# The rows of h and the middle tiles shifted by 32 bytes against the weights, in a two-layer hybrid trunk

## The chip, the cores and the metric

The kernel runs on one core of a Trainium2 chip. The metric is device time in microseconds (us), measured over several executions of which the median counts; one further execution is recorded by the hardware profiler, and all profile lines come from that one. The engines are called as in the profile: PE (TensorE, matmuls), PEld (TensorE, loading of weights), DVE (VectorE), ACT (ScalarE), POOL (GpSimd) and SP (SyncE, which here issues the DMAs).

## The reference

The model has two layers, 256 tokens and a width of 2048. Layer 0 mixes tokens by retention with 8 heads, layer 1 by a short gated convolution; each is followed by a SwiGLU feed-forward part with 5632 middle columns. Every sub-layer is normed, scaled and shifted by columns that come from a vector c, and its output is gated and added to x.

```python
for i in range(DEPTH):
    mod = (c_act @ w_mod[i] + b_mod[i])[:, None, :]
    sh1, sc1, g1, sh2, sc2, g2 = jnp.split(mod, 6, axis=-1)
    h = (rms_norm(x, norm1_g[i]) * (1.0 + sc1) + sh1).astype(x.dtype)
    ...
    x = (x + g1 * y).astype(x.dtype)
    h = (rms_norm(x, norm2_g[i]) * (1.0 + sc2) + sh2).astype(x.dtype)
    x = (x + g2 * swiglu(h, ffn_w_in[i], ffn_w_out[i])).astype(x.dtype)
return rms_norm(x, final_g).astype(x.dtype)
```

Everything is float32: h @ w for the input projections, then the mixer, then a second product with the output weights. In retention, q and k are rotated by their position before the scores: `concatenate([t1 * cos - t2 * sin, t2 * cos + t1 * sin])`.

## The kernel before

**Layout.** Activations are held transposed: 128 partitions carry 128 of the 2048 columns, and the 256 tokens lie along the free dimension. h is one tile of 16 rows (L481); row k holds columns 128k to 128k+127 in two planes of 256 values, the rounded value and the rest that rounding left. A plane takes S + 2 = 258 floats, since two more columns carry the shift during a norm. So a row is 2 x 258 x 4 = 2,064 bytes long, which is 16 more than a multiple of 128.

**Products.** Each float32 weight is also split in two, hi and lo, by `prepare` (L297): ACT casts hi from the raw weights (L312), DVE subtracts to get lo (L315), 1024 columns at a time, into 4 buffers each (L310, L311). `product` (L347) multiplies one 128x128 block of weights by one row: hi times both planes (512 columns, L357), then lo times the first plane (256 columns, L360). This is called a pair below. `packed` (L376) does the same with three matmuls of 256 columns (L397 to L399); `by_token` (L367) keeps a slice of a row of h as the weights and moves 512 columns of hi or lo through it (L372 to L374); `normed` (L493) uses 258 columns (L516 to L518), for the first 6 blocks of columns after each norm.

**Middle tiles.** The results of the first product of a sub-layer are kept as middle tiles of 2 x 256 values, 2,048 bytes each: `rm_tile` (L619) in retention, `mid` in the feed-forward part (L948) and in the convolution (L969). The output product `output` (L540) reads them in place of h.

**Where these lie.** In the program's allocation every hi and lo buffer begins 32 bytes past a multiple of 128, and so do h, the retention's middle tiles and the later ones. A block of weights takes 512 bytes of a partition in a buffer. So a middle tile stands at 0 bytes from the weights modulo 128, and row k of h at 16k modulo 128: rows 0 and 8 at 0, rows 2 and 10 at 32, rows 4 and 12 at 64, and so on.

**Order.** PE's order is the program's; in the first stage that of DVE and ACT is as well (L691, L785). Weights come by 1 MB DMAs on SP's queue in the order of use (`fetch`, L291), between them those for the columns from c (L238). The retention starts with four spans (L758, L786, L788, L795), in which `packed` runs over some of the rows for one or two heads while the rows of h and the columns from c are still being made; after a span its banks are copied or added to by `held` (L623), 8 of them in turn. Then each head is finished (`projections`, L915): `pair` (L899) does the rows that are left and adds what was held into a tile `qs`, `rope` (L804) rotates q and k, `values`, `scores` (with a decay table loaded by a DMA, L834) and `gate` follow. The feed-forward parts and the convolution are loops over blocks of columns; `summed` (L405) adds the two halves of a bank by way of a small tile `low` that ACT writes, and the closure `total` in `normed` (L529) uses `low` too.

Of the kernel before, what the change touches and what calls it, by code (L numbers as in the profile page):

```python
# [10 lines left out]
F32 = mybir.dt.float32  # L11
# [6 lines left out]
P = 128  # L18
# [30 lines left out]
STEPS = (8, 8, 20)  # L49
RAW_BUFS = 3  # L50
PART_BUFS = 4

Q0, K0, V0, G0 = 0, HEADS * DK, 2 * HEADS * DK, 2 * HEADS * DK + HEADS * DV
SH1, SC1, GT1, SH2, SC2, GT2 = range(6)
# [133 lines left out]
def trunk(ctx: ExitStack, tc: tile.TileContext, x_in, c_in, pos_in, w_mod, cols_in, tab_in, w_all, out):  # L188
# [8 lines left out]
    def name(s):  # L197
        serial[0] += 1
        return f"{s}_{serial[0]}"
# [203 lines left out]
        return banks  # L403

    def summed(pt, dst=None, at=slice(0, S)):  # L405
        low = tmp("low", bufs=3)
        nc.scalar.copy(low[:, at], pt[:, 1, at])
        dst = tmp("sum", bufs=4) if dst is None else dst
        nc.vector.tensor_tensor(dst, pt[:, 0, at], low[:, at], op=ALU.add)
        return dst  # L410
# [67 lines left out]

    hpool = ctx.enter_context(tc.tile_pool(name="hpool", bufs=1))

    h_all = hpool.tile([P, KT, 2, S + 2], F32R, tag="h", name="h")  # L481
    h = [h_all[:, j, :, :S] for j in range(KT)]

    def scaled_only(layer, norm, j):
# [8 lines left out]
    def normed(accs, layer, norm, g):  # L493

        needed(layer, SH2 if norm else SH1)
        shift = mod_s[layer][norm].unsqueeze(2).to_broadcast([P, KT, 2])  # L500
        ends = [h_all[:, :, i, S:] for i in range(2)]
        nc.scalar.copy(ends[0], shift)
        nc.vector.tensor_tensor(ends[1], shift, ends[0].bitcast(F32), op=ALU.subtract)
        banks = [bank().rearrange("p a b -> p (a b)")[:, : S + 2] for _ in g.cols]
        made = [0]

        def more(n):
            while made[0] < n:
                modulated(h[made[0]], made[0], root, layer, norm)
                made[0] += 1  # L510

        for k in g.ks:
            rows = [h_all[:, k, i, :] for i in range(2)]
            for c, pt in zip(g.cols, banks):
                hi, lo = take(g, k, c)
                nc.tensor.matmul(pt, hi, rows[0], start=k == 0, stop=False)  # L516
                nc.tensor.matmul(pt, hi, rows[1], start=False, stop=False)  # L517
                nc.tensor.matmul(pt, lo, rows[0], start=False, stop=k == KT - 1)  # L518
            if k == ROOTS_AT:
                r = norm_roots(norm_sums(accs), D)  # L520
            elif k == SPREAD_AT:
                root = tmp("rb", bufs=1)
                nc.scalar.copy(root, norm_spread(r))
            elif k > SPREAD_AT:
                more(min(k, made[0] + 2))
        more(KT)
        paced(len(g.cols) * len(g.ks))

        def total(pt, dst=None):  # L529
            end = tmp("end", (P, 1), bufs=2)  # L530
            nc.scalar.copy(end, pt[:, S : S + 1])
            t = tmp("low", bufs=3)
            nc.vector.tensor_tensor(t, pt[:, :S], root, op=ALU.mult)
            dst = tmp("sum", bufs=4) if dst is None else dst
            nc.scalar.activation(dst, t, AF.Identity, bias=end)
            return dst

        return [lambda dst=None, pt=pt: total(pt, dst) for pt in banks]
# [27 lines left out]
    with ExitStack() as inner:  # L566
# [64 lines left out]
        with tc.tile_pool(name="start", bufs=1) as sp:  # L631
# [59 lines left out]
            with tc.manual_schedule(engines={mybir.EngineType.DVE, mybir.EngineType.Activation}):  # L691
                c_row = sp.tile([1, D], F32, tag="raw", name=name("raw"), bufs=START_RAWS)
                nc.sync.dma_start(c_row, c_in)
                for i in range(4):
                    nc.sync.dma_start(x4[i], x_in[:, 4 * i : 4 * i + 4, :])
                loaded(SC1, 0)
                nc.sync.dma_start(cols, cols_in)
                loaded(SH1, 0)
                nc.sync.dma_start(tab, tab_in[:, : 1 + P])
                fetch()  # L700
                nc.scalar.activation(half, half, AF.Silu)
                nc.vector.memset(half, -0.5)
                eps = const.tile([P, 1], F32, tag="eps", name="eps")
                nc.vector.memset(eps, EPS)
                ahead_of(1)

                spread_c = []
                for i in range(0, D, 2 * S):
                    pt = bank().rearrange("p a b -> p (a b)")
                    nc.tensor.matmul(pt, ones[0:1, :], c_row[:, i : i + 2 * S], start=True, stop=True)  # L710
                    spread_c.append(pt)

                def silu(i):
                    nc.scalar.activation(cb[:, 2 * S * i : 2 * S * i + 2 * S], spread_c[i], AF.Silu)

                def square(i):

                    sq = [rm.tile([P, 2, S], F32, tag=f"mid{2 * i + n}", name=name("sq")) for n in range(2)]
                    for n in range(2):
                        nc.scalar.activation(sq[n], x4[i][:, 2 * n : 2 * n + 2, :], AF.Square)  # L720
                    return sq

                def added(a, b):
                    for n in range(2):
                        nc.vector.tensor_tensor(a[n], a[n], b[n], op=ALU.add)

                acc = square(0)
                for i in range(1, 4):
                    added(acc, square(i))
                for i in range(4):  # L730
                    silu(i)
                nc.vector.tensor_tensor(acc[0], acc[0], acc[1], op=ALU.add)
                nc.vector.tensor_tensor(acc[0][:, 0, :], acc[0][:, 0, :], acc[0][:, 1, :], op=ALU.add)
                pt = norm_sums([acc[0][:, 0, :]])
                reduced(SC1, 0)
                gain_1 = const.tile([P, KT], F32, tag="gain1", name="gain1")
                nc.vector.scalar_tensor_tensor(
                    gain_1, b_mod[:, SC1 * KT : (SC1 + 1) * KT], 1.0, gain[0][0], op0=ALU.add, op1=ALU.mult
                )
                reduced(SH1, 0)  # L740
                mean = tmp("rs", (P, 2), bufs=4)
                nc.scalar.activation(mean, pt[:, 0, 0:2], AF.Identity, bias=eps, scale=1.0 / D)
                first_cols = [column(SC1, 0)]
                r = tmp("rs", (P, 2), bufs=4)
                nc.gpsimd.tensor_tensor(r, mean, half, op=ALU.pow)
                rb = tmp("rb", pool=sp, bufs=1)
                nc.scalar.copy(rb, norm_spread(r))
                norm_two(0)
                first_cols.append(column(SH1, 0))

                banks = [bank() for _ in range(8)]

                def before(k):
                    low = []
                    prepare(lambda: low.append(row(k)))
                    low[0]()

                pts = packed(RET_SPANS[0], h, before=before, between=both_reduced, banks=banks)  # L758
                prepare()
                prepare()  # L760
                for i, pt in enumerate(pts):
                    held(divmod(i, 4), pt)
# [20 lines left out]
                )  # L783

            with tc.manual_schedule(engines={mybir.EngineType.DVE, mybir.EngineType.Activation}):  # L785
                for i, pt in enumerate(span(RET_SPANS[1])):  # L786
                    held((2 + i // 4, i % 4), pt)
                pts = span(RET_SPANS[2])  # L788
                for i, pt in enumerate(pts):
                    if i < 4:  # L790
                        held(divmod(i, 4), pt)
# [9 lines left out]

        rp = inner.enter_context(tc.tile_pool(name="rpool", bufs=1))

        def rope(s, tag):  # L804
            a = tmp("qa", (P, 2, S), pool=rp, bufs=1)
            nc.vector.tensor_tensor(a, s, cos.unsqueeze(1).to_broadcast([P, 2, S]), op=ALU.mult)
            b = tmp("qb", (P, 2, S), pool=rp, bufs=1)
            nc.vector.tensor_tensor(b[:, 0, :], s[:, 1, :], sin, op=ALU.mult)
            nc.vector.tensor_tensor(b[:, 1, :], s[:, 0, :], sin, op=ALU.mult)
            nc.vector.tensor_tensor(a[:, 0, :], a[:, 0, :], b[:, 0, :], op=ALU.subtract)  # L810
            nc.vector.tensor_tensor(a[:, 1, :], a[:, 1, :], b[:, 1, :], op=ALU.add)
            dst = rp.tile([P, 2, 2, S], F32R, tag=tag, name=name(tag))
            nc.scalar.copy(dst[:, 0, :, :], a)
            nc.vector.tensor_tensor(dst[:, 1, :, :], a, dst[:, 0, :, :].bitcast(F32), op=ALU.subtract)
# [15 lines left out]
            return v  # L830

        def scores(head, q, k):
            decay = rp.tile([P, S], F32, tag="decay", name=name("decay"), bufs=1)
            nc.sync.dma_start(decay, tab_in[:, 1 + P + head * S : 1 + P + (head + 1) * S])  # L834
            both = []
            for jt in range(2):
# [76 lines left out]
            return sums  # L913

        def projections(head):  # L915
            q = rope(*pair(head, 0), "q")
            k = rope(*pair(head, 1), "k")
            v = values(head, RET_HEADS[head][1])
            sp = scores(head, q, k)
            sg = [gate(s) for s in pair(head, 2)]  # L920
# [130 lines left out]
```

## Time and profile before

| what | before |
|---|---|
| median of 3 runs | 2644.53 us (2642.65 to 2645.33) |
| the profiled execution, its own time | 2641.89 us |
| its span (first to last instruction) | 2640.1 us |
| PE busy | 2608.1 us, 99% of the span, 15220 matmuls |
| PEld busy | 2291.2 us, 87% |
| DVE busy | 1990.3 us, 75% |
| ACT busy | 1244.8 us, 47% |
| HBM read | 682.99 MB, 259 GB/s over the span |
| granted TensorE clock | 0.998 on average |

The span is what the profile divides up; the profiled execution's own time is 1.8 us more, and the median of the runs 2.6 us more than that. Groups of instructions are given as line, engine, operation, what is written <- what is read, shape, number, and then busy time and the mean length of one. The lengths of matmuls overlap: a matmul's recorded length (some 0.39 us for 512 columns) holds a pipeline's depth, and what one of them costs PE is the distance between its start and the next one's.

### The profile page before, as it was taken

The page shows a single profiled execution, that of the slowest core. Times are in us where ns is not written, and L with a number is a line of the kernel's source. Part 1 is how long each engine was busy: PE and PEld are TensorE (multiplying, and loading weights), DVE is VectorE, ACT ScalarE, POOL GpSimd, SP SyncE. Part 2 cuts the span into 40 slices and gives each one's busy share as a digit, 9 for nine tenths or more (in the row PEclk, how much of TensorE's full clock was granted, in tenths as well). Part 3 has the DMA queues.
Part 4 walks back from the last instruction along what each step waited for, and adds up shares of the span by engine and source line. Part 5 has one row for each costly group of instructions (what it writes and reads, how often), then busy time and mean ns, then how long its engine had stood idle before and what let it go on. Part 6 is the DMA issues. An engine that isn't in the chain of part 4 may idle for free.

```text
span 2640.1 us, 38225 instructions
## 1 busy us (share of the span) xinstructions
PE 2608.1 (99%) x15220; PEld 2291.2 (87%) x15220; DVE 1990.3 (75%) x2543; ACT 1244.8 (47%) x1770; POOL 146.6 (6%) x230
## 2 busy tenths in 40 slices
PE   7999999999999999999999999999999999999998
PEld 5888889888889888888888898888988888888887
DVE  7998878777698877777777888888886765555554
ACT  5644443444455444344444454444554443444443
POOL 0000001010000011110100001100000000000000
PEclk9999999999999999999999999999999999999999
DMA  9976668776686877777777768777677655555553
GB/s 397 391 273 256 258 242 317 258 271 259 251 300 243 314 283 272 273 283 283 287 270 282 268 224 321 280 281 262 253 277 263 248 219 191 190 191 187 183 190 127
DMA packets 96950, 687.58 MB, mean 260 GB/s; under 512 B 10753, under 2 KB 12545, under 8 KB 13825
## 3 DMA queue, kind: packets, MB, share of 16 engines
q1 hardware_dynamic: 96770, 685.13, 70.0%
q8 instruction: 119, 1.95, 0.3%
q14 instruction: 61, 0.50, 0.1%
HBM read 682.99 MB, written 2.10 MB: 259 GB/s over the span
## 4 chain that ended last, share of the span: by engine, by line
PE 76%; issue 19%; DVE 2%; DMA 1%; ACT 1%; POOL 0%; DVEq 0%; POOLq 0%; ACTq 0%
PE bank L357 35%; PE bank L360 18%; PE bank L372 4%; PE bank L373 4%; PE bank L374 4%; PE bank L399 2%; PE bank L398 2%; PE bank L397 2%; PE bank L517 1%; PE bank L516 1%; PE bank L518 1%; DVE raw L642 1%; DMA raw<-w_all 1%; PE bank L869 1%; DVE lo L315 1%
## 5 line engine op out<-in xcount | busy, mean ns | idle before, releaser
L315 DVE TENSOR_TENSOR lo<-raw,hi 128x1024 fp32r<-128x1024 f32 x912 | 1111.5, 1222 | 551.6 <-ACT hi L312 549.3
L312 ACT CAST hi<-raw 128x1024 fp32r<-128x1024 f32 x912 | 953.2, 1050 | 1088.9 <-PE bank L357 649.0
L357 PE MATMUL bank<-h,hi 128*128 128x512 f32 x3296 | 1155.2, 395 | 0.0
L360 PE MATMUL bank<-h,lo 128*128 128x256 f32 x3296 | 924.4, 280 | 0.0
L357 PEld LDWEIGHTS bank<-h,hi 128*128 128x128 f32 x3296 | 622.6, 189 | 145.3
L360 PEld LDWEIGHTS bank<-h,lo 128*128 128x128 f32 x3296 | 622.0, 189 | 0.0
L357 PE MATMUL bank<-mid,hi 128*128 128x512 f32 x1604 | 556.3, 393 | 0.0
L360 PE MATMUL bank<-mid,lo 128*128 128x256 f32 x1604 | 444.9, 277 | 0.6 <-DVE lo L315 0.6
L246 DVE SCALAR_TENSOR_TENSOR raw<-raw,cb 128x2048 f32<-128x2048 f32 x160 | 365.4, 2284 | 11.7 <-DMA raw<-w_mod 11.3
L357 PEld LDWEIGHTS bank<-mid,hi 128*128 128x128 f32 x1604 | 300.7, 187 | 69.4
L360 PEld LDWEIGHTS bank<-mid,lo 128*128 128x128 f32 x1604 | 301.3, 188 | 0.9 <-DVE lo L315 0.9
L372 PE MATMUL bank<-hi,h 128*128 128x512 f32 x512 | 202.7, 396 | 0.0
L373 PE MATMUL bank<-lo,h 128*128 128x512 f32 x512 | 201.9, 394 | 0.0
L374 PE MATMUL bank<-hi,h 128*128 128x512 f32 x512 | 201.9, 394 | 0.0
L357 PE MATMUL bank<-rm,hi 128*128 128x512 f32 x496 | 174.2, 396 | 0.0
L399 PE MATMUL bank<-h,lo 128*128 128x256 f32 x512 | 145.6, 284 | 9.1 <-DVE lo L315 9.1
L397 PE MATMUL bank<-h,hi 128*128 128x256 f32 x512 | 144.9, 283 | 2.5 <-ACT h L670 2.5
L398 PE MATMUL bank<-h,hi 128*128 128x256 f32 x512 | 144.8, 283 | 0.5 <-DVE h L671 0.5
L360 PE MATMUL bank<-rm,lo 128*128 128x256 f32 x496 | 138.5, 279 | 0.0
L374 PEld LDWEIGHTS bank<-hi,h 128*128 128x128 f32 x512 | 96.3, 188 | 22.7
L372 PEld LDWEIGHTS bank<-hi,h 128*128 128x128 f32 x512 | 96.6, 189 | 19.6
L373 PEld LDWEIGHTS bank<-lo,h 128*128 128x128 f32 x512 | 96.4, 188 | 19.6
(152 smaller groups left out, 2239.3 us busy)
## 6 DMA issues: line engine op xcount, KB each, us to landing
raw<-w_all SPq DMA_DIRECT2D x456, 1024.0 KB, 4.8
raw<-w_mod SPq DMA_DIRECT2D x192, 1024.0 KB, 5.0
x<-x_in SPq DMA_DIRECT2D x4, 512.0 KB, 5.7
out<-out SPq DMA_DIRECT2D x5, 256.0 KB, 3.4
decay<-tab_in SPq DMA_DIRECT2D x8, 128.0 KB, 2.2
out<-out SPq DMA_DIRECT2D x3, 128.0 KB, 2.5
out<-out SPq DMA_DIRECT2D x1, 384.0 KB, 2.7
cols<-cols_in SPq DMA_DIRECT2D x1, 160.0 KB, 8.8
```

The costliest lines, as they stand in the source:

```text
L246: nc.vector.scalar_tensor_tensor(raw, raw, 1.0, cb, op0=ALU.mult, op1=ALU.mult, accum_out=total)
L312: nc.scalar.copy(hi, raw)
L315: nc.vector.tensor_tensor(lo, raw, hi.bitcast(F32), op=ALU.subtract)
L357: nc.tensor.matmul(pt, hi, h, start=fresh and k == g.ks[0], stop=False, skip_group_check=True)
L360: nc.tensor.matmul(pt[:, 1, :], lo, h[:, 0, :], start=False, stop=last and k == g.ks[-1], skip_group_check=True)
L372: nc.tensor.matmul(o, ht[:, 0, :], hi, start=first, stop=False)
L373: nc.tensor.matmul(o, ht[:, 0, :], lo, start=False, stop=False)
L374: nc.tensor.matmul(o, ht[:, 1, :], hi, start=False, stop=last)
L397: nc.tensor.matmul(pt, hi, h[:, 0, :], start=first, stop=False, skip_group_check=True)
L398: nc.tensor.matmul(pt, hi, h[:, 1, :], start=False, stop=False, skip_group_check=True)
L399: nc.tensor.matmul(pt, lo, h[:, 0, :], start=False, stop=last, skip_group_check=True)
L516: nc.tensor.matmul(pt, hi, rows[0], start=k == 0, stop=False)
```

## The change

h's rows become 2 x 288 floats, 2,304 bytes, a multiple of 128 (`PAD = 32`); a tile of 8 floats, `aside`, is allocated ahead of h and not used, so that h and all that is allocated behind it in the same order begin 32 bytes later. With that, every row of h and every middle tile is at 32 bytes from the weights modulo 128. The two shift columns stay at 256 and 257 of a plane; the rest of the padding is not read.

Room for it comes from smaller temporaries: two `low` buffers for three; `rb` in a pool where a tile of that name exists already; `decay` in one of the three `u` buffers in place of a tile of its own; no tile `qb` in `rope`, where both products with sin are now one instruction over 512 values, written in place over s where s is a tile (or a bank) that was made ahead, otherwise into `qs`. Finally `prepare()` is called once more behind the second and the third span, ahead of the `held` calls, so that one more half buffer of weights is split before the banks are emptied.

```diff
+PAD = 32
...
     def summed(pt, dst=None, at=slice(0, S)):
-        low = tmp("low", bufs=3)
+        low = tmp("low", bufs=2)
...
-    h_all = hpool.tile([P, KT, 2, S + 2], F32R, tag="h", name="h")
+    hpool.tile([P, 8], F32, tag="aside", name="aside")
+    h_all = hpool.tile([P, KT, 2, S + PAD], F32R, tag="h", name="h")
     h = [h_all[:, j, :, :S] for j in range(KT)]
...
-        ends = [h_all[:, :, i, S:] for i in range(2)]
+        ends = [h_all[:, :, i, S : S + 2] for i in range(2)]
...
-            rows = [h_all[:, k, i, :] for i in range(2)]
+            rows = [h_all[:, k, i, : S + 2] for i in range(2)]
...
-            t = tmp("low", bufs=3)
+            t = tmp("low", bufs=2)
...
-                rb = tmp("rb", pool=sp, bufs=1)
+                rb = tmp("rb", bufs=1)
...
-                for i, pt in enumerate(span(RET_SPANS[1])):
+                pts = span(RET_SPANS[1])
+                prepare()
+                for i, pt in enumerate(pts):
                     held((2 + i // 4, i % 4), pt)
                 pts = span(RET_SPANS[2])
+                prepare()
                 for i, pt in enumerate(pts):
...
-        def rope(s, tag):
+        def rope(s, tag, ours):
+
             a = tmp("qa", (P, 2, S), pool=rp, bufs=1)
             nc.vector.tensor_tensor(a, s, cos.unsqueeze(1).to_broadcast([P, 2, S]), op=ALU.mult)
-            b = tmp("qb", (P, 2, S), pool=rp, bufs=1)
-            nc.vector.tensor_tensor(b[:, 0, :], s[:, 1, :], sin, op=ALU.mult)
-            nc.vector.tensor_tensor(b[:, 1, :], s[:, 0, :], sin, op=ALU.mult)
-            nc.vector.tensor_tensor(a[:, 0, :], a[:, 0, :], b[:, 0, :], op=ALU.subtract)
-            nc.vector.tensor_tensor(a[:, 1, :], a[:, 1, :], b[:, 1, :], op=ALU.add)
+            b = s if ours else tmp("qs", (P, 2, S), pool=rp, bufs=1)
+            nc.vector.tensor_tensor(b, s, sin.unsqueeze(1).to_broadcast([P, 2, S]), op=ALU.mult)
+            nc.vector.tensor_tensor(a[:, 0, :], a[:, 0, :], b[:, 1, :], op=ALU.subtract)
+            nc.vector.tensor_tensor(a[:, 1, :], a[:, 1, :], b[:, 0, :], op=ALU.add)
...
-            decay = rp.tile([P, S], F32, tag="decay", name=name("decay"), bufs=1)
+            decay = tmp("u", bufs=3)
...
-            q = rope(*pair(head, 0), "q")
-            k = rope(*pair(head, 1), "k")
+            q = rope(*pair(head, 0), "q", (head, 0) in ahead)
+            k = rope(*pair(head, 1), "k", (head, 1) in ahead)
```

## The prediction

> **What bounds the kernel now.** I read the page's busy times first, then the chain that ended last, then the costliest groups and PE's waits, and at last the order of time inside two columns of blocks.
>
> ```profile
> PE 2608.1 (99%) x15220; PEld 2291.2 (87%) x15220; DVE 1990.3 (75%) x2543; ACT 1244.8 (47%) x1770; POOL 146.6 (6%) x230
> PE 76%; issue 19%; DVE 2%; DMA 1%; ACT 1%; POOL 0%; DVEq 0%; POOLq 0%; ACTq 0%
> L357 PE MATMUL bank<-h,hi 128*128 128x512 f32 x3296 | 1155.2, 395 | 0.0
> L357 PE MATMUL bank<-mid,hi 128*128 128x512 f32 x1604 | 556.3, 393 | 0.0
> L357 PE MATMUL bank<-rm,hi 128*128 128x512 f32 x496 | 174.2, 396 | 0.0
> PE bank L399 <- DVE lo L315: 9.1, 6, 2.3
> ```
>
> PE works through the whole span and its waits are small (the longest total is 9.1 us, all in the first 160 us). So the time is the number of matmuls by the distance between their starts. The table of windows says how far this holds: from 190 to 2500 us PE is busy without a break but for 0.6 us, while DVE is busy 1749 of these 2310 us and the DMA engines 0.53 to 0.76 of the time. From 0 to 190 us DVE is busy 166 us and the DMA share is 0.88 to 0.97; a faster PE gains nothing there.
>
> The distances are in the order of time. First rows 0 to 11 of one column of blocks on h, then eight pairs on middle tiles (start in us, length, group; most lines between are left out):
>
> ```profile
> 1700.64 0.39 PE L357 MATMUL bank<-h,hi 128*128 128x512 f32 x1
> ...
> 1700.98 0.39 PE L357 MATMUL bank<-h,hi 128*128 128x512 f32 x1
> ...
> 1701.33 0.39 PE L357 MATMUL bank<-h,hi 128*128 128x512 f32 x1
> ...
> 1701.68 0.39 PE L357 MATMUL bank<-h,hi 128*128 128x512 f32 x1
> ...
> 1702.37 0.40 PE L357 MATMUL bank<-h,hi 128*128 128x512 f32 x1
> ...
> 1703.08 0.40 PE L357 MATMUL bank<-h,hi 128*128 128x512 f32 x1
> ...
> 1703.44 0.40 PE L357 MATMUL bank<-h,hi 128*128 128x512 f32 x1
> ...
> 1704.14 0.40 PE L357 MATMUL bank<-h,hi 128*128 128x512 f32 x1
> 1704.37 0.29 PE L360 MATMUL bank<-h,lo 128*128 128x256 f32 x1
> 1704.50 0.40 PE L357 MATMUL bank<-h,hi 128*128 128x512 f32 x1
> ```
>
> ```profile
> 1500.26 0.40 PE L357 MATMUL bank<-mid,hi 128*128 128x512 f32 x1
> ...
> 1503.03 0.40 PE L357 MATMUL bank<-mid,hi 128*128 128x512 f32 x1
> ```
>
> A pair on h takes 0.34 us in row 0 and 0.36 in rows 7 and 10. The same row takes the same time in every column: taken to the nanosecond over 206 columns, rows 0 to 15 last 342, 350, 349, 343, 347, 356, 353, 357, 348, 355, 356, 349, 348, 351, 357 and 346 ns, each within some 2 ns of itself; their mean is 350.4. Buffers of weights, banks and the work of the other engines change all the time meanwhile, so none of them makes the difference; what belongs to a row is its address. On middle tiles, which all stand alike to the weights, the 8 pairs take 2.77 us, and over longer stretches a pair takes 346.7 throughout. The retention's middle tiles stand alike too and show 347 in one half and 353 in the other (mean 350), so one alignment can settle in more than one rhythm. The first matmuls, at 19 to 24 us, follow each other at 427 ns for 512 columns and 213 for 256, in every row alike; half of that, 320 for a pair, is what a matmul would take later if nothing were added.
>
> **The change part by part.** *Rows and middle tiles at 32 bytes.* It touches 3296 pairs on h, 1604 on mid and 496 on rm, and the same rows in the matmuls of 256, 258 and 512 columns beside. No row of the trace has this state (a constant 32), so I bound it. From below: the shortest distances that occur are 224 ns for 512 columns (by-token, last row) and 112 for 256 (row 0); all pairs at 336 would give 14.4 x 3296 + 10.7 x 1604 + 14 x 496 = 47 + 17 + 7 = 71 us, by-token matmuls 8 x 1200 = 10, the other 256s at 112 for 119 another 7 x 1950 = 14: 95 us less. From above: all pairs as slow as row 7, 357, would cost 6.6 x 3296 + 10.3 x 1604 + 7 x 496 = 22 + 17 + 3 = 42 us. I take the value of the best row, 342 for every pair, since the constant alignments seen (347 mostly) lie at the low end of the rows and a distance of 32 keeps the two reads apart where 0 lays them on one another: 8.4 x 3296 = 27.7, 4.7 x 1604 = 7.5 and 8 x 496 = 4.0 us. By-token matmuls follow each other at 224 to 240 ns, mean 232; at 226 the 1200 that come after the spans give 7.2. The 256s of `packed` after the spans (some 1090, 119 ns each) at 116 give 3.3, the 864 of `normed` (120 ns) at 117 2.6. Together 52 us. The matmuls of the spans count for nothing, for DVE sets the pace there.
>
> The Trainium skill, in "TensorE: Matmul & The Clock Gate", Step-by-step, has PE read the moving operand and the next weights through two independent ports, so that loading weights takes nothing from a running matmul; its distance of N/2.4 + 2.5 ns would make a pair 325, an estimate by that page, and some 130 us of today's pairs would be avoidable. This case's rows disagree: no pair is below 342, and addresses do matter.
>
> *One more prepare() behind two spans.* PE waits for lo at 109.2 us (0.4) and 151.9 us (2.2), shortly behind these span ends, where DVE does the held adds (0.68 us each) and sums of 2.28 first. Preparing earlier takes away between nothing and these 2.6 us; I take 2. The ACT cast put ahead (1.05) delays the first `held` copy; that bank gets its last matmul some 5 us before its span ends, and is needed again only behind the end, so the cast lies under the span's last row.
>
> *rope.* Two DVE products of 0.41 become one over 512 values, 0.69 like the one with cos: 0.13 less, 16 times, 2 us of DVE, hidden under PE's matmuls for the rest of k and for v; from 190 to 790 us DVE is busy 484 of 600, so the path gets nothing of it. Written in place, `qs` stays in use two DVE instructions longer (0.83), but its next writer is DVE itself, so no wait.
>
> *Smaller temporaries.* With two `low` buffers ACT's copy (365 ns) waits for the add (417) of two copies ago. Blocks of columns come 5.6 us apart, so it is long done; after a norm six come in one burst, paced by ACT (504) with DVE (416) behind. The worst, 0.1 x 18, stays under PE's 5.6 us per block: nothing. The decay load would wait for a `u` buffer; the first is issued at 173.2 and takes the buffer read last at 155.7, so SP's queue (behind it raw weights) isn't held up, and later ones follow loads three heads back. `rb` has no other user until the next norm.
>
> Sum: 52 + 2 = 54 us off. The profiled execution's 2641.9 is 2.6 below the median; its own time would come to 2641.9 - 54 = 2588, the median to 2644.5 - 54 = **2590 us**.
>
> **Rivals.**
>
> *Alike, but no lower.* Every row of h takes what a middle tile takes now, 346.7; the distance itself does nothing. For it speaks that the constant alignment is what the trace shows; against it, that rows differ by more than a rhythm would. h gains 3.7 x 3296 = 12.2 us, with the waits 14.2: 2630.
>
> *32 bytes is a bad distance.* Rows 2 and 10 stand at 32 today and take 349 and 356, mean 352.8; rows at 0 take 345, rows at 64 347. If the alignment then holds the slower rhythm in all rows, h costs 2.4 x 3296 = 7.9, mid 6.1 x 1604 = 9.8, rm 2.8 x 496 = 1.4, by-token some 1.5 x 1200 = 1.8, less 2 for the waits: 19 us, 2664. Against it: a row's time also hangs on the rows before it (rows 8 and 0 stand alike and differ by 6 ns), so rows 2 and 10 say little of a constant 32. It decides from a mean pair of about 349.8, the present mean of all pairs (349.3) and the 2 us of waits. At row 7's 357 it would be 2685.
>
> *The address does nothing.* The pattern over the rows would come from something else that repeats with them, and only the waits are left: 2642. The sameness over 206 columns and the middle tiles' other value speak against it. The Trainium skill's rule above ("TensorE: Matmul & The Clock Gate", Step-by-step) would have it so.
>
> **How the numbers follow.** Low pairs 0.42, alike but no lower 0.22, a bad distance 0.28, no effect 0.08. This kernel's measurement tells 0.2%, 5.3 us, from no change. The first two are faster: 0.64; same 0.08; slower 0.28. The likeliest alone runs from 2550 (all at the shortest distances, 95 us) to 2630. For 8 in 10 the range starts at 2545 and reaches over the bad distance at rows 2 and 10 with 4 us more, to 2668; beyond lie about 0.1 on the slow side and as much below.
>
> **What would show it.** The 16 rows of a column on h take one time, or alternate between two, with no pattern by row; a column takes 16 x 342 = 5.47 us (5.61 now), and 8 pairs on mid 2.74 (2.77). The waits at 109 and 152 us are gone, and PE stays at 99%, DVE's busy time within 5 us. I am wrong if mid pairs are longer than 346.7 or a column on h is over 5.61 us; or if pairs get shorter and the time doesn't, with PE waiting for lo or for raw weights in the middle of the span.

## The result and the profile after

| | before | after |
|---|---|---|
| median of 16 runs each, side by side | 2643.22 us (2640.61 to 2648.71) | 2649.05 us (2647.03 to 2652.97) |
| ratio after / before | | 1.0022, 95% interval 1.0014 to 1.0030 |
| the profiled execution, its own time | 2641.89 us | 2648.87 us |
| its span | 2640.1 us | 2647.0 us |
| granted TensorE clock | 0.998 | 0.997 |

The change makes the kernel slower by 5.8 us, 0.2%, where 54 us less were forecast. The page of the profile after, first the busy times, then the chain that ended last, then the three groups of 512 columns (busy time, mean ns of one, idle before):

```profile
PE 2615.0 (99%) x15220; PEld 2301.0 (87%) x15220; DVE 1989.4 (75%) x2527; ACT 1245.6 (47%) x1770; POOL 149.9 (6%) x230
PE 76%; issue 19%; DVE 2%; DMA 2%; ACT 1%; POOL 0%; DVEq 0%; ACTq 0%; POOLq 0%
L358 PE MATMUL bank<-h,hi 128*128 128x512 f32 x3296 | 1160.4, 395 | 0.0
L358 PE MATMUL bank<-mid,hi 128*128 128x512 f32 x1604 | 556.4, 390 | 0.0
L358 PE MATMUL bank<-rm,hi 128*128 128x512 f32 x496 | 172.5, 390 | 0.0
```

(Lines of the code have moved by one: L358 and L361 are the pair, L357 and L360 before; L398 to L400 are `packed`, L397 to L399 before.) The bound is the same: PE at 99%, the same chain, as many matmuls. PE is busy 6.9 us longer, which is the whole difference of the spans, and the group on h alone took 5.2 us of that, while rm gave 1.7 back. So the loss lies where the change was aimed: in the distances between starts on h.

The order of time on h, as shown of before (start in us, length, group; lines between left out). The last line is one column of 16 pairs behind the first:

```profile
1700.30 0.40 PE L358 MATMUL bank<-h,hi 128*128 128x512 f32 x1
1700.65 0.39 PE L358 MATMUL bank<-h,hi 128*128 128x512 f32 x1
...
1701.71 0.40 PE L358 MATMUL bank<-h,hi 128*128 128x512 f32 x1
1702.06 0.40 PE L358 MATMUL bank<-h,hi 128*128 128x512 f32 x1
...
1705.93 0.39 PE L358 MATMUL bank<-h,hi 128*128 128x512 f32 x1
```

and eight pairs on middle tiles:

```profile
1500.11 0.39 PE L358 MATMUL bank<-mid,hi 128*128 128x512 f32 x1
...
1502.88 0.39 PE L358 MATMUL bank<-mid,hi 128*128 128x512 f32 x1
```

A column on h takes 5.63 us (5.61 before), eight pairs on mid 2.77 as before. Taken to the nanosecond from the starts in the trace, the pattern over the rows is gone: all 16 rows have the same mean, 352.0 ns, in a rhythm that repeats after five pairs (1760 ns; the last but one of the lines stands five pairs behind the first). Middle tiles stay at 346.7 and the retention's go from 350.2 to 346.7, now without its slower half. Below, "a pair" is always this mean from start to start, without the few pairs that hold a wait.

The waits of PE (instruction <- what it waited for: us in all, times, longest) and the window from 190 to 800 us:

```profile
PE bank L400 <- DVE lo L316: 6.9, 4, 2.3
...
PE bank L398 <- DVE rm L628: 0.8, 1, 0.8
...
PE bank L874 <- ACT sp L415: 0.6, 1, 0.6
...
PE bank L874 <- DVE sp L416: 0.5, 1, 0.5
```

```profile
190.00:800.00 610.00, 608.91 (x3442) 530.95 (x3441) 490.25 (x626) 281.11 (x388) 49.55 (x75) 1.00 0.73 265
```

The wait for lo fell from 9.1 us to 6.9, but three waits are new: 0.8 for a bank that `held` had not emptied (at 145 us) and 1.1 for the first head's scores (at 219 us). In the window PE was busy 610.00 of 610 us before; 1.1 us are missing now (second number).

The 6.9 us between the spans, added up from the starts with the waits in them: pairs on h +5.2, by-token matmuls +2.7 (1.0 of it the new wait at 145 us), the 258-column matmuls of `normed` +1.5, the matmuls behind the scores +1.0, pairs on rm -1.7, `packed` -0.8, the rest -1.0.

### The profile page after: what moved, and what is told of

It reads as the page before. It is cut to its first block, busy times and chain, and to the rows that moved or that the text cites. A ratio compares the mean times of both kernels' runs of the same rounds, so it can differ in the third digit from the quotient of the medians.

```text
span 2647.0 us, 38396 instructions
## 1 busy us (share of the span) xinstructions
PE 2615.0 (99%) x15220; PEld 2301.0 (87%) x15220; DVE 1989.4 (75%) x2527; ACT 1245.6 (47%) x1770; POOL 149.9 (6%) x230
## 4 chain that ended last, share of the span: by engine, by line
PE 76%; issue 19%; DVE 2%; DMA 2%; ACT 1%; POOL 0%; DVEq 0%; ACTq 0%; POOLq 0%
PE bank L358 34%; PE bank L361 18%; PE bank L373 4%; PE bank L374 4%; PE bank L375 4%; PE bank L400 2%; PE bank L399 2%; PE bank L398 2%; PE bank L518 1%; PE bank L519 1%; PE bank L520 1%; DMA raw<-w_all 1%; DVE raw L644 1%; PE bank L874 1%; DVE lo L316 1%
## 5 line engine op out<-in xcount | busy, mean ns | idle before, releaser
L358 PE MATMUL bank<-h,hi 128*128 128x512 f32 x3296 | 1160.4, 395 | 0.0
L361 PE MATMUL bank<-h,lo 128*128 128x256 f32 x3296 | 925.2, 281 | 0.0
L358 PEld LDWEIGHTS bank<-h,hi 128*128 128x128 f32 x3296 | 618.3, 188 | 150.3
L361 PEld LDWEIGHTS bank<-h,lo 128*128 128x128 f32 x3296 | 618.6, 188 | 0.0
L358 PE MATMUL bank<-mid,hi 128*128 128x512 f32 x1604 | 556.4, 390 | 0.0
L361 PE MATMUL bank<-mid,lo 128*128 128x256 f32 x1604 | 452.4, 282 | 0.6 <-DVE lo L316 0.6
L358 PEld LDWEIGHTS bank<-mid,hi 128*128 128x128 f32 x1604 | 301.1, 188 | 63.1
L361 PEld LDWEIGHTS bank<-mid,lo 128*128 128x128 f32 x1604 | 303.1, 189 | 0.9 <-DVE lo L316 0.9
L358 PE MATMUL bank<-rm,hi 128*128 128x512 f32 x496 | 172.5, 390 | 0.0
L400 PE MATMUL bank<-h,lo 128*128 128x256 f32 x512 | 145.9, 285 | 6.9 <-DVE lo L316 6.9
L398 PE MATMUL bank<-h,hi 128*128 128x256 f32 x512 | 145.3, 284 | 3.3 <-ACT h L672 2.5
L399 PE MATMUL bank<-h,hi 128*128 128x256 f32 x512 | 145.3, 284 | 0.5 <-DVE h L673 0.5
L361 PE MATMUL bank<-rm,lo 128*128 128x256 f32 x496 | 139.8, 282 | 0.0
```

Of the source, the lines that this page charges most:

```text
L358: nc.tensor.matmul(pt, hi, h, start=fresh and k == g.ks[0], stop=False, skip_group_check=True)
L361: nc.tensor.matmul(pt[:, 1, :], lo, h[:, 0, :], start=False, stop=last and k == g.ks[-1], skip_group_check=True)
L398: nc.tensor.matmul(pt, hi, h[:, 0, :], start=first, stop=False, skip_group_check=True)
L399: nc.tensor.matmul(pt, hi, h[:, 1, :], start=False, stop=False, skip_group_check=True)
L400: nc.tensor.matmul(pt, lo, h[:, 0, :], start=False, stop=last, skip_group_check=True)
```

## The experiments

Three theories stood at the beginning. **A**: the place of the rows decides, and in it the walk of the moving read, which jumps 128 bytes from the first plane to the second since `PAD = 32` widened the gap between them (from 8 bytes); the distance to the weights is second to that. **B**: 32 bytes is a bad distance. **C**: the other parts of the change cost the time. A place is given below as the distance of the first plane from the weights (in bytes, modulo 128) and the gap between the planes: h after the change is 32/128, a middle tile 0/0 before and 32/0 after, row k of h before 16k/8.

### The same rows at distance 0

```diff
-    hpool.tile([P, 8], F32, tag="aside", name="aside")
```

> The changed kernel without the tile aside: rows of h stay 2304 bytes long, but every row and every middle tile is back at 0 bytes from the weights modulo 128. Theory A (a pair's time is set by the whole path of its moving operand against the weights, so the jump of 128 bytes between the two planes of a row, which only h has, is what makes h slower than mid): pairs on h near 352 ns again, all 16 rows alike, mid at 346.7, time within 3 us of the changed kernel's 2649. Theory B (the distance modulo 128 is what counts): h at 0 takes what mid took at 0, 346.7, which is 17 us less than the changed kernel, about 2632. Theory C (the smaller temporaries and the moved prepare cost the time): 2649 as well, but with h below 350.

2645.76 us, ratio to before 1.0005 (0.9996 to 1.0014). Pairs on h take 350.0 on average (349.4 to 350.6 over the rows), on mid 350.6, on rm 350.7. B would have had h at 346.7 and falls. A is half right: with the 128-byte gap h stays slow at distance 0 too, but it is 350.0 and not 352. The 350.6 on mid is a mean of two values: 353.3 in three stages and 346.7 in two, where before, also at distance 0, all five stages had 346.7. So distance 0 doesn't hold one value even without a gap; at 32, in the change, all five had 346.7.

### The planes of a row without a gap, at distance 32

The shift columns go ahead of the first plane and behind the second; `normed` reads them as windows over either end.

```diff
-    h_all = hpool.tile([P, KT, 2, S + PAD], F32R, tag="h", name="h")
-    h = [h_all[:, j, :, :S] for j in range(KT)]
+    ROW, FRONT = 576, 32
+    h_all = hpool.tile([P, KT * ROW], F32R, tag="h", name="h")
+    h_rows = h_all[:, : KT * ROW].rearrange("p (k r) -> p k r", r=ROW)
+    h = [h_all[:, j * ROW + FRONT : j * ROW + FRONT + 2 * S].rearrange("p (a b) -> p a b", a=2) for j in range(KT)]
...
-            rows = [h_all[:, k, i, : S + 2] for i in range(2)]
+            rows = [h_rows[:, k, FRONT - 2 : FRONT + S], h_rows[:, k, FRONT + S : FRONT + 2 * S + 2]]
...
```

(The lines left out put the banks of `normed` and its closure `total` right for the moved shift columns; `total` has one small ACT instruction and one small tile more.)

> The changed kernel with the two planes of a row of h laid one directly behind the other (the shift's two columns stand ahead of the first plane and behind the second), rows still 2304 bytes long and at 32 bytes from the weights. Theory A: pairs on h go to mid's 346.7 ns in all rows, 5.3 ns x 3296 = 17 us less than the changed kernel: about 2632, 0.4% under the kernel before. Theory B: nothing but the distance counts, so h stays at 352 and the time at 2649.

2630.63 us, ratio to before **0.9951 (0.9938 to 0.9963)**: faster than both kernels. Its groups on h (page) and a column of 16 pairs (order of time):

```profile
L358 PE MATMUL bank<-h,hi 128*128 128x512 f32 x3296 | 1142.9, 392 | 0.0
```

```profile
1699.87 0.39 PE L358 MATMUL bank<-h,hi 128*128 128x512 f32 x1
...
1705.42 0.39 PE L358 MATMUL bank<-h,hi 128*128 128x512 f32 x1
```

A column takes 5.55 us, a pair 346.7 on h, mid and rm alike. 5.3 ns less on 3296 pairs are 17.5 us; the medians lie 18.4 apart. A's forecast came, B's 352 didn't: the gap between the planes is what made h slow at distance 32. The small tile also moves the weights, which by this program's allocation begin 96 bytes past a multiple of 128 instead of 32; h's rows begin at a multiple of 128 here and 64 bytes past one in the change. As middle tiles take 346.7 in both, and 351.5 where they begin at a multiple of 128 but 96 bytes from the weights (96/0 below), it is the distance to the weights that a place has to be given by, not the address alone.

### The other parts alone, with the rows of before

```diff
-    hpool.tile([P, 8], F32, tag="aside", name="aside")
-    h_all = hpool.tile([P, KT, 2, S + PAD], F32R, tag="h", name="h")
+    h_all = hpool.tile([P, KT, 2, S + 2], F32R, tag="h", name="h")
```

> The changed kernel with the rows of before (258 floats a plane, no tile aside, all else as changed). Theories A and B: the 16 values of the rows come back, mean pair 350.4 on h, and the time falls by about 5 us of matmuls on h plus 2 to 3 us of other matmuls on h less 2 us on the retention's middle tiles, to 2642 to 2645. Theory C: the time stays at 2648 to 2650, since the smaller temporaries and the moved prepare are what costs.

2644.43 us, ratio 1.0006 (0.9998 to 1.0015): C falls: no gain or loss of the temporaries and the two `prepare()` calls together shows. The pattern of rows is back to within 1 ns of before (mean 350.4), so that pattern does belong to the place of the rows.

### Lengths of the two matmuls, at distance 0

```diff
+                n = 64 if mode[0] == "narrow" and not (fresh and k == g.ks[0]) else P
+                m = 64 if mode[0] in ("narrow", "narrow lo") else P
...
-                    pt, hi, h, start=fresh and k == g.ks[0], stop=False, skip_group_check=True
+                    pt[:n], hi[:, :n], h, start=fresh and k == g.ks[0], stop=False, skip_group_check=True
...
+                if mode[0] == "both":
+                    nc.tensor.matmul(pt, lo, h, start=False, stop=last and k == g.ks[-1], skip_group_check=True)
+                elif mode[0] != "hi":
+                    nc.tensor.matmul(
+                        pt[:m, 1, :], lo[:, :m], h[:, 0, :], start=False, stop=last and k == g.ks[-1],
...
+            mode[0] = {0: 'both', 1: 'narrow lo', 4: 'hi', 2: 'narrow', 3: None}.get(2 * layer + part)
```

> Other lengths in four output products, at distance 0 on middle tiles (so 346.7 ns a pair today): layer 0 part 0 multiplies lo by both planes (more work, 1024 columns a pair); layer 0 part 1 loads only 64 columns of lo (half of lo's part left out); the convolution's leaves the lo matmul out; layer 1 part 0 loads only 64 columns of hi and lo; layer 1 part 1 is as before. If the extra over 2.4 columns per ns belongs to the weight loads (13.3 ns for each load of 128 columns): 453 ns, 340, 227 for the single matmul, 333, and 347. If it goes with the columns that are moved (a twelfth of their time): 462, 347, 231, 347 and 347.

Order of time, first lo over both planes (six pairs from the first line to the last), then hi and lo with 64 columns of weights (nine pairs):

```profile
1060.02 0.39 PE L361 MATMUL bank<-mid,hi 128*128 128x512 f32 x1
1060.24 0.39 PE L365 MATMUL bank<-mid,lo 128*128 128x512 f32 x1
...
1062.74 0.39 PE L361 MATMUL bank<-mid,hi 128*128 128x512 f32 x1
```

```profile
2189.89 0.39 PE L361 MATMUL bank<-mid,hi 128*64 128x512 f32 x1
...
2192.95 0.39 PE L361 MATMUL bank<-mid,hi 128*64 128x512 f32 x1
```

The one run took 2676.98 us; what it is for are the distances. Two matmuls of 512 columns take 453.4 ns, 226.7 each; a lone hi takes 226.7 too where no wait follows. So 256 more columns cost 453.4 - 346.7 = 106.7, 2.4 columns per ns, and each of these matmuls takes 13.3 ns on top, at 512 columns as at 256: 320 + 2 x 13.3 = 346.7. With 64 columns of weights in lo a pair is 340.0, with 64 in both it is 340.0 as well; 333 were expected, a miss: halving hi's weights brought nothing. So the extra isn't fixed, but that the loading of weights makes it isn't shown: with 64 columns of weights a matmul also writes only 64 partitions of its bank, and the run doesn't tell the two apart. The Trainium skill ("TensorE: Matmul & The Clock Gate", Step-by-step) says that loading the next weights takes no read bandwidth from the running matmul. The 6.7 ns that the narrower lo saves, at unchanged moving columns, would speak against it only if they come from the load.

### Other distances for middle tiles without a gap

```diff
+    PLACES = {0: (4, 0), 1: (12, 0), 4: (16, 0), 2: (24, 0), 3: (28, 0)}
...
+        at, gap = PLACES[place]
+        t = mpool.tile([P, 544], F32R, tag=f"mid{i}", name=name("mid"))
+        return t[:, at : at + 2 * (S + gap)].rearrange("p (a b) -> p a b", a=2)[:, :, :S]
```

(The numbers are in floats of 4 bytes. A like edit, with other numbers and slices, serves the two runs with gaps. The middle tiles also become longer, 2176 bytes here and 2304 in those runs, against 2048; what that does by itself was not tried, but 32/0 has 346.7 with rows of 2048 and of 2304 bytes.)

> Before's rows of h and the other parts of the change; the middle tiles keep their two planes contiguous but lie at another distance to the weights in each stage: 16 bytes in the first layer's first part, 48 in its second, 64 in the convolution, 96 in the second layer's first part, 112 in its second. Theory A (what counts is how the moving read walks, not how far it lies from the weights): about 346.7 ns for a pair in all five, with nothing below; at most a slower rhythm of 353 where the two reads fall badly. Theory B (the distance sets a pair, so that one distance gives 342 as in the first row of h before): one of the five below 344 and one above 350. The rows of h are to repeat the pattern of before, 342 to 357, since nothing of them is changed. Total about 2644 by A, up to 5 us less by B.

Pairs: 349.4 at 16/0, 351.2 at 48/0, 350.6 at 64/0, 351.5 at 96/0, 350.2 at 112/0. Neither theory had this: no place at 342 as B's extension wanted, and none at A's 346.7. Without a gap the distance still counts, and of seven distances only 32 keeps 346.7 throughout. These are means of a stage, and each stage here begins otherwise than it goes on: in its first 40 to 60 pairs, where several columns of blocks take turns at each row, 16/0 takes 345.1 and then 350.0, 64/0 takes 352.2 and then 350.0. The time of this one run, 2651.17, is some 7 us over the 2643.9 of before; 3.9 ns on 1604 pairs make 6.3.

### Gaps between the planes of middle tiles

> Before's rows of h and the other parts of the change; the middle tiles get a gap between their two planes: 8 bytes in the first layer's first part, 32 in its second, 64 in the convolution, 128 in the second layer's first part, all four with the first plane at distance 0, and 32 bytes with the first plane at distance 32 in the second layer's second part. Theory A (the jump from one plane to the other costs): the pairs with 128 bytes at about 350 to 352, as the rows of h at pitch 1152 had it; those with 8 bytes, the gap that the rows of before have, between 342 and 357 with their place, which for one distance makes one number for all middle tiles alike; 32 and 64 bytes not known, over 346.7 if any jump costs. Rival (a jump costs only where it is a whole 128 bytes, so that both planes fall on one place): 346.7 for 8, 32 and 64. If the second plane's place alone set a pair, 8 bytes at distance 0 would repeat row 0 of h before, 342.

Pairs: 353.3 at 0/8, 346.7 at 0/32, 348.9 at 0/64 (346.7 before a wait in the stage, 350.0 behind it), 350.0 at 0/128, 353.3 at 32/32; the one run took 2657.39 us. A has 128 bytes right, but not that any jump costs, for 32 bytes at distance 0 cost nothing. The rival falls with 353.3 at 8 bytes, and the second plane's place alone doesn't set a pair, or 0/8 would have 342. The 0/128 repeats to 0.1 ns what h had there in the first experiment. The first place is the one that matters for the prediction, here as two starts eight pairs apart, 2.83 us:

```profile
1099.70 0.40 PE L358 MATMUL bank<-mid,hi 128*128 128x512 f32 x1
...
1102.53 0.40 PE L358 MATMUL bank<-mid,hi 128*128 128x512 f32 x1
```

0/8 is the place of row 0 of h before, which took 342 there. When every middle tile stands so, a pair takes 353.3.

### Without the moved prepare()

```diff
                 pts = span(RET_SPANS[1])
-                prepare()
                 for i, pt in enumerate(pts):
...
                 pts = span(RET_SPANS[2])
-                prepare()
```

> The change with contiguous planes, without the two calls of prepare that were moved ahead. If the move gained 1.1 us at 152 us and gave it back at 145 and 219, as the waits of TensorE showed, the time is that of the run with contiguous planes within 1.5 us (2629 to 2632). If the move was worth the 2 us that the prediction gave it: 2632.5 or more. If it costs: 2629 or less.

2630.59 us, ratio to before 0.9947 (0.9934 to 0.9961), against 2630.63 with the two calls: no gain of the move shows. Of its waits:

```profile
PE bank L400 <- DVE lo L316: 7.1, 6, 2.2
...
PE bank L876 <- DVE sp L416: 0.5, 1, 0.5
PE bank L876 <- ACT sp L415: 0.4, 1, 0.4
```

The wait for the bank of `held` at 145 us is gone with the calls, and the one for lo at 152 is back at 2.0 us. The wait for the scores at 219 stays, and it is there with the rows of before as well (0.8 us in the run with the other parts alone), so that one comes from the other parts of the change, neither from `prepare()` nor from the rows; which of them (`rope` in place, `decay`, `low`) was not tried.

### No gap, at distance 0

```diff
-    hpool.tile([P, 8], F32, tag="aside", name="aside")
```

(against the version without gaps)

> The change with contiguous planes, but rows of h and middle tiles at distance 0 instead of 32 (the aside tile left out). If the distance is worth nothing once the planes are contiguous: pairs at 346.7, time 2629 to 2632. If at distance 0 the slower three-pair rhythm of 353 takes over in part, as on rm before and on the middle tiles at distance 0: pairs at 348 to 353 on average, which is 1.3 to 6.3 ns more on some 5,100 pairs, 2637 to 2662.

2655.75 us, ratio 1.0042 (1.0029 to 1.0055): 25 us above the same kernel at distance 32. Pairs take 351.1 on h, 352.7 on mid and 347.6 on rm, together (4.4 x 3296 + 6.0 x 1604 + 0.9 x 494) 24.6 us. On mid four stages have 353.3 throughout; the fifth shows two rhythms at the same place, one after the other (the convolution):

```profile
1809.30 0.40 PE L358 MATMUL bank<-mid,hi 128*128 128x512 f32 x1
...
1811.77 0.40 PE L358 MATMUL bank<-mid,hi 128*128 128x512 f32 x1
...
1832.26 0.40 PE L358 MATMUL bank<-mid,hi 128*128 128x512 f32 x1
1833.05 0.38 PE L361 MATMUL bank<-mid,lo 128*128 128x256 f32 x1 [0.40 <-DVE lo L316]
...
1849.92 0.39 PE L358 MATMUL bank<-mid,hi 128*128 128x512 f32 x1
...
1852.35 0.39 PE L358 MATMUL bank<-mid,hi 128*128 128x512 f32 x1
```

Seven pairs in 2.47 us, then seven in 2.43 us: 353.3 and 346.7 by the starts to the nanosecond. The switch falls on the wait of PE for lo at 1833 us. The run with the other parts alone has a switch in the same stage at 1829 us, the other way, from 346.7 to 353.3, where a matmul with lo also starts 0.19 us late. Before, at the same place, the stage has such a wait (0.6 us) and 346.7 on both sides of it. So a pause of PE can be where the rhythm changes; that it makes the change was not tested. At 32/0 the same stage has waits of 0.6 to 1.1 us in four kernels (the change, contiguous planes with and without the two calls, and h with its first plane at 0 below) and 346.7 on both sides each time.

### Distance 32 for each row, with the 8-byte gap of before

```diff
-    h_all = hpool.tile([P, KT, 2, S + PAD], F32R, tag="h", name="h")
+    GAP, FRONT, ROW = 2, 0, 544
+    h_flat = hpool.tile([P, KT * ROW], F32R, tag="h", name="h")
+    h_rows = h_flat[:, : KT * ROW].rearrange("p (k r) -> p k r", r=ROW)
+    h_all = h_rows[:, :, FRONT : FRONT + 2 * (S + GAP)].rearrange("p k (a b) -> p k a b", a=2)
```

> The change with one thing altered: the two planes of a row of h lie 8 bytes apart, as before, instead of 128, and the rows are 2176 bytes from one another, so that every row stays at distance 32. The middle tiles stay contiguous at distance 32 (346.7 ns). Theory D (the walk of the moving read as a whole, first plane's place and gap together, sets the rhythm, and an 8-byte gap breaks it as it did on the middle tiles at distance 0): pairs on h of 350 to 354, 2640 to 2656 us. Rival (only the jump of a whole 128 bytes costs, and a fixed distance of 32 does the rest): pairs of 346.7, 2630 to 2633 us. Rival of the prediction (each row at the best row's number): 342, about 2614 us.

2651.99 us, ratio 1.0028 (1.0017 to 1.0038). A column of 16 pairs takes 5.65 us, 353.3 a pair on average; mid and rm stay at 346.7:

```profile
1699.87 0.40 PE L358 MATMUL bank<-h,hi 128*128 128x512 f32 x1
...
1705.53 0.40 PE L358 MATMUL bank<-h,hi 128*128 128x512 f32 x1
```

For h this is the idea of the change with nothing else in it, one distance for all rows and planes apart as they were, and it costs 2.9 ns a pair against the mixed rows of before. Though all rows have one place, they don't take one time: in every column the even rows take 356.6 ns and the odd ones 350.0. So a single row's time isn't the number of its place modulo 128; whether the neighbours make it, or that even and odd rows lie 128 bytes apart modulo 256, is open.

### First plane at 0, the second 32 bytes behind it

The edit is that of the last run with `GAP, FRONT, ROW = 8, 24, 576`.

> The change with the rows of h moved: first plane at distance 0, the second 32 bytes behind its end (rows 2304 bytes from one another), which is the place where the middle tiles of the first layer's second part kept 346.7 ns in the run with gaps. The middle tiles themselves stay contiguous at distance 32. If a place has its own number, the same for rows of h as for middle tiles: pairs on h of 346.7, 2630 to 2633 us. If the number hangs on what runs around it (the order of the products, the phase in which a stage begins): 348 to 353, 2635 to 2652 us.

2630.46 us, ratio 0.9945 (0.9929 to 0.9962), pairs on h at 346.7. What the middle tiles showed at 0/32 carried over to h, in another stage and with another order of rows. It is also the shorter edit of the two that make the kernel faster, since `normed` stays as it is.

### Is it the second plane's place?

> Before's rows of h and the other parts of the change; on the middle tiles five more places whose second plane always begins 32 bytes off a multiple of 128, as it does in the two places that kept 346.7 ns in every stage (first plane at 32 with no gap, first plane at 0 with a gap of 32 bytes): first plane at 16 with a gap of 16 bytes in the first layer's first part, at 24 with 8 in its second, at 64 with 96 in the convolution, at 32 with 128 in the second layer's first part (the very place that the rows of h have in the change), at 96 with 64 in the second layer's second part. Theory E (the second plane's place decides): 346.7 in all five. Theory D (the whole walk counts, with no simple rule): the fourth near 352.0, which is what the rows of h have there, the others between 346.7 and 354 each with its own number.

Pairs: 346.7 at 16/16, 360.0 at 24/8, 349.1 at 64/96, 352.0 at 32/128, 350.0 at 96/64; the one run took 2651.68 us. The longest, and the fourth place, as starts eight pairs apart:

```profile
1450.05 0.40 PE L358 MATMUL bank<-mid,hi 128*128 128x512 f32 x1
...
1452.92 0.40 PE L358 MATMUL bank<-mid,hi 128*128 128x512 f32 x1
```

```profile
2200.10 0.39 PE L358 MATMUL bank<-mid,hi 128*128 128x512 f32 x1
...
2202.91 0.40 PE L358 MATMUL bank<-mid,hi 128*128 128x512 f32 x1
```

The first is 24/8, 2.87 us; the second 32/128, 2.81 us, the place and the 352.0 of h in the change, in the same rhythm of five pairs. Theory E falls. D has the fourth right, but not that the others stay under 354. The 349.1 at 64/96 is a mean of 353.3 and, from 1831 us on, 346.7. So D holds in a weak form: where a place keeps one mean, it is the same for h and mid as far as both were tried (32/0, 0/32, 0/128, 32/128); some places have two, and no simple rule was found.

All places together (the mean over a stage; where the rhythm changed within a stage, the two values in brackets). Most places were seen in one stage of one run:

| place of every row or tile | pair in ns | where seen |
|---|---|---|
| 32/0 | 346.7 | mid, rm after; h, mid, rm without gaps |
| 0/32 | 346.7 | mid; h |
| 16/16 | 346.7 | mid |
| 0/0 | 346.7 to 353.3 (each alone, or one after the other; h 351.1) | mid, rm before; h, mid, rm |
| 0/64 | 348.9 (346.7, then 350.0) | mid |
| 64/96 | 349.1 (353.3, then 346.7) | mid |
| 16/0 | 349.4 (345.1, then 350.0) | mid |
| 0/128 | 350.0 | h; mid |
| 96/64 | 350.0 | mid |
| 112/0 | 350.2 | mid |
| 64/0 | 350.6 (352.2, then 350.0) | mid |
| 48/0, 96/0 | 351.2, 351.5 | mid |
| 32/128 | 352.0 | h after; mid |
| 0/8, 32/32 | 353.3 | mid |
| 32/8 | 353.3 (even rows 356.6, odd rows 350.0) | h |
| 24/8 | 360.0 | mid |

## Why the prediction was wrong

**The bound and the place of the effect** were right: PE's distances set the time, the pattern over the rows comes from where they lie, and nearly all of the difference came out of the groups on h, mid and rm. So was the form: "the 16 rows of a column on h take one time", with no pattern by row. Its own sign of being wrong came: a column on h takes 5.63 us, over 5.61.

**The step that failed** is "I take the value of the best row, 342 for every pair, since the constant alignments seen (347 mostly) lie at the low end of the rows and a distance of 32 keeps the two reads apart where 0 lays them on one another". It has two faults, both shown. First, a row's number was taken for a number of its place. Row 0's place given to every row of a stage makes 353.3 (mid at 0/8), not 342, and rows that all stand at 32/8 still take 356.6 and 350.0 in turn. The prediction itself noted that rows 0 and 8 stand alike and differ by 6 ns, but used that only against a rival. Second, only the distance of the first plane was looked at. The change also widened the gap between planes from 8 bytes to 128, and that was costed nowhere: at the same distance of 32 a pair takes 346.7 without a gap, 352.0 with 128 bytes and 353.3 with 8. So the term of 27.7 us gained on h was a loss of 5.2; mid's 7.5 was nothing (0.1 more); rm's 4.0 was 1.7 (its first half was at 347.9 before, its second at 353.3).

**The lower end**, all pairs at 336, reached under what any of the places allowed. Over a stage a pair takes at least 320 + 2 x 13.3 = 346.7 in all of them; over a shorter stretch 345.1 was seen, in the first 40 pairs at 16/0.

**By-token, `packed` and `normed`**, 7.2 + 3.3 + 2.6 us: by-token matmuls behind the spans stayed at 233 ns, and the 258s went from 121 to 123 (hi and lo together). The 256s of `packed` on h stayed near 119; the 228 on mid and rm did go from 119.8 to 116.7, close to the 116 of the prediction, which is 0.7 us of the 3.3. On h the terms were the same step on other shapes and fell with it.

**The two prepare() calls**, 2 us: the waits shortly behind these spans (109 and 152 us before) fell from 2.5 to 1.0 us in all (from start to start, less a matmul's own 0.12), where the sign said gone. But "the cast lies under the span's last row" failed: PE waited 0.8 us for DVE's add of a held bank at 145, and in the run with the other parts alone 1.2 us there for ACT's cast. Without the calls the time is the same.

**rope, temporaries and decay**, nothing: right as far as the run can tell (1.0006, 0.9998 to 1.0015, together with `prepare()`), though some 1.1 us of new waits for the first head's scores belong here. The decay load now lands 4.5 us after its issue (2.2 before); no wait of PE for it appears.

**The rivals.** "Alike, but no lower" had the right value for mid and rm, and for h as soon as the gap is gone (2630 forecast, 2630.63 and 2630.46 measured in the two versions). That the time agrees so closely is in part luck: it counted 2 us of waits that didn't come and left out the 1.7 us of rm that did. "32 bytes is a bad distance" was right in sign and names a time 15 us too high. For rows of h at 32 with the 8-byte gap its 352.8, from rows 2 and 10, is near the 353.3 measured; but mid and rm, for which it used the same number, have no gap and stayed at 346.7. That was luck too, for the rows at 0 took 345 by the same reading, and 0/8 made 353.3. The distance isn't the cause: 32 is the best of the seven tried for planes without a gap, and the kernel without gaps is 25 us faster there than at 0. "The address does nothing" is out. What stays open is why a place has its number, and what picks one where it has two: no trace shows the reads themselves.

## What to carry to other kernels

If one group of matmuls shows several distances between starts that repeat with the operand's row, don't take the best row as the price of its address: give one whole stage that place, in a single run with a different place in each stage, and read the mean, and whether it stays the same from the stage's beginning to its end. A padding that moves rows also changes the jump inside a row; cost both, and put padding at the end of the row or measure the gap. Two places (32/0 and 0/32) kept the best number here in every stage and run, and were worth 0.5%.

## What the runs showed of the hardware

- Addresses of the moving rows, with the same instructions, move a pair of 512 and 256 columns between 346.7 and 360.0 ns, up to 4%. Where a place keeps one mean, it repeats to 0.1 ns in another stage and another kernel (352.0 at 32/128, 350.0 at 0/128).
- One place can have two rhythms. At 0/0 one stage went from 353.3 to 346.7 ns in its middle and one, in another kernel, from 346.7 to 353.3, each at a pause of PE (0.4 us idle at 1833 us; 0.19 us late at 1829 us). At 32/0 the faster one came in every stage of five kernels, through pauses of 0.6 to 1.1 us too.
- In a pair at 346.7, or in two matmuls of 512 columns (453.4), each matmul costs 13.3 ns over its columns at 2.4 per ns. Three 256s in a row (`packed` on mid) come to the same 13 ns at 0/0 (119.8 each) and to 10 at 32/0 (116.7). At the start, around 21 us, 256 columns follow each other at 213 ns, 1.2 columns per ns, with no extra left.
